# First Strassen pair: T3's split ahead of T1's, its convolution next and the gelu behind; a head's last norms and transposes behind the next key projection

## The chip, the cores and the metric

The kernel runs on one core of one Trainium2 chip. The metric is the time of one execution in device microseconds; the time before is the median of three runs. Its engines are called PE (TensorE, matmuls), DVE (VectorE), ACT (ScalarE), POOL (GpSimd) and SP (SyncE, which only issues transfers here). Each engine works through its own list of instructions in order, and waits by semaphores for the others.

## The reference

One layer of a decoder with a hybrid mixer, for a prompt of 1024 tokens and for 8 sample sequences of 8 tokens each; the width is 1024, D_FF is 2816.

```python
h  = rmsnorm(x, pre_mix_g)
proj = h @ w_in                                   # q, k, v, gates of 4 retention and 4 mLSTM heads
ret_y = head_groupnorm(retention(q_r, k_r, v_r), ret_g) * silu(g_r)
ml_y  = head_groupnorm(mlstm(q_m, k_m, v_m, gates), ml_g) * sigmoid(o_m)
x = x + rmsnorm(concat(ret_y, ml_y) @ w_out, post_mix_g)
up = rmsnorm(x, pre_ffn_g) @ w_up                 # 2 * D_FF columns
conv = sum(padded[:, j:j + L] * conv_w[j] for j in range(3)) + conv_b    # causal, each column alone
gate, val = conv[..., :D_FF], conv[..., D_FF:]
x = x + rmsnorm((gelu(gate) * val) @ w_down, post_ffn_g)
```

The new states of the heads and the last rows of the convolution are outputs too.

## The kernel before

**Numbers.** Every operand of a big matmul is split in two parts, high (h) and low (l), and a product is the sum of three matmuls: high by high, high by low and low by high. A split is two instructions: ACT writes the high part (line 148), DVE the low part as a difference (line 150). So a weight `wh_up`/`wl_up` costs ACT and DVE one instruction each, and T1 to T4, sums of activations, are split in the same way in two halves each (`T1h`, `T1l`, ...).

**The heads.** `mix_head` works through the heads r0 to r3 (retention) and m0 to m3 (mLSTM). It projects the head's q, k (and v) first: `proj` computes four blocks of tokens, 24 matmuls each (line 164), in one of two PSUM banks in turn, and an evacuation by ACT or DVE empties each. Then come nine chunks of 128 tokens in the order `[[0, 1], [2, 3], [4, 5], [6, 7], [8]]`; chunk 8 holds the sample's tokens. `stats` gathers mean and variance, and `finish` closes a group of four chunks, or the sample: it computes the norm's factors, scales each chunk on DVE (line 682, `on_...`), transposes it on PE (line 684, `yt_...`) and evacuates it into `yT`. Each `finish` is called one step late. So the group of chunks 4 to 7 is finished behind the sample's step, and the sample's at the head's end; both were called ahead of the next head's projections.

**The order.** A scheduler merges the program as it is written into a list for each engine, when the kernel is built: where an instruction has to wait, others that come later in the text can be set ahead of it. `tc.issue_after(x)` binds an instruction behind x. The order is then fixed. It also picks which of a pool's PSUM banks a tile gets.

**The up-projection.** Columns of `w_up` are worked on in pairs j = 0 to 21: a gate tile (`Ug`) and a value tile (`Uv`). Pairs 0 and 1 (`firsts`, `plain`) are plain products. From pair 2 on, each pair is a Strassen-Winograd scheme of seven products (`prods`), with two halves of 12 matmuls each, in the order A11, A12, S2, S1, S4, S3, A22, times the activations B1, B2, T2, T1, B3, T3, T4 (lines 1079 to 1081; the trace names them `up_A` or `up_S` by the weight). Each half takes one of eight PSUM banks (`psF`). A11's are evacuated by ACT into `Uv` (line 1064), the others by DVE's additions into `Ug` and `Uv` (lines 1053 and 1057). The U tiles are double buffered: pair 2 writes into pair 0's, so its evacuations wait until pair 0's convolution has read them.

**What follows a pair.** `convs` convolves `Ug`, applies the gelu on ACT (line 1098; the first one needs a table load, as other functions were in use) and convolves `Uv`. A convolution is an ACT instruction (line 1092) and two DVE passes (line 1094), each for the prompt (1024 elements) and the sample (64). `pair_out` multiplies gate by value (`act`, line 1103) and sends it away (`bd`); every second pair, differences on GpSimd (line 1111) are sent too.

**Around the change.** The products A11 and A12 of pair 2 are issued first (`held`), while the activations are still summed. Then the text has the splits of T2 and T1, a weight, the convolutions of pair 0, the split of T3, the other weights, T4, and the outputs of pairs 0 and 1, before the loop over pairs from 2 on. `last["acc"]` and `last["sq"]` name the DVE and ACT instruction behind which the next splits are bound.

Of the kernel before, what the change touches and what calls it, by code (L numbers as in the profile page):

```python
# [16 lines left out]
P = 128  # L17
# [79 lines left out]
def hybrid_layer_kernel(ctx: ExitStack, tc: tile.TileContext, a: dict, o: dict):  # L97
# [63 lines left out]
    def product(ps, w, x, b, k, term):  # L161

        u, v = ((w[0], 0), (w[1], 0), (w[0], 1))[term]
        nc.tensor.matmul(ps, u[:, k * P:(k + 1) * P], x[b // 2][k // 4][v][:, k % 4, qcols(b)],  # L164
                         start=k == term == 0, stop=k == KT - 1 and term == 2)

    def dense(ps, w, x, b):

# [367 lines left out]

    EARLY = (0, 1, 2, 3)
    turns = {"wq": 0}
    early = []

    def mix_head(hd, ml):

# [10 lines left out]
        if ml:  # L553
            proj((16 + hd, evac_norm(q, 1.0)))
            proj((20 + hd, evac_norm(k, SCALE)))
            proj((24 + hd, evac_copy(v)))
        else:
            eq, ek = evac_rot(q, f"q{nm}"), evac_rot(k, f"k{nm}")
            if hd == 0:
                proj((0, eq), mid=pre_norm, banks=lambda i, b: psB)  # L560
                proj((NH, ek))
            else:
                proj((hd, eq))
                proj((NH + hd, ek))
            if hd == 0:
                token_norms()
                yT.extend(flat("yT", i, k=2) for i in range(4))
            if hd > 1:
                proj((2 * NH + hd, evac_copy(v)))
            if hd == 0:  # L570
                gate_proj()
                for _ in range(5):
                    next(rows)
                for i in range(NH):
                    proj((12 + i, early_gate(i)), banks=lambda i, b: psB if b % 2 else psA)
                    next(rows)
# [80 lines left out]
                nc.vector.bn_stats(st, on[:, i, :P])  # L657
                nc.vector.bn_aggr(mv[:, i, :], st)

        def finish(on, mv, c0, L, name):  # L660

            sh = [P, L]
            small = lambda tag: m2.tile([P, 4], F32, tag=tag, name=f"{tag}_{name}")[:, :L]
# [17 lines left out]
            for i in range(L):  # L681
                nc.vector.tensor_scalar(on[:, i, :P], on[:, i, :P], mv[:, i, 0:1], A[:, i:i + 1],
                                        ALU.subtract, ALU.mult)
                nc.tensor.transpose(ps[:, i * P:(i + 1) * P], on[:, i, :P], ident)
# [9 lines left out]
        def sample(kz, vt, qs, pt):  # L694
# [28 lines left out]
            nc.sync.dma_start(o["cs" if ml else "ss"][hd].rearrange("p (s v) -> p s v", s=NB), sb[:, :, :P])  # L723
            if ml:
                nc.sync.dma_start(o["ns"][hd], sb[:, :, P])
            return lambda: finish(on, mv, 8, 1, f"{nm}s")

        S = None
        g = math.exp(CH * LG[hd])
# [2 lines left out]
        def pair_of(c0, kz, vt, qs, pt):  # L732
# [23 lines left out]
                S = S2  # L756
            stats(on, po, c0 % 4, 2, mv, f"{nm}{c0}")
            if c0 % 4 == 2:
                return lambda: finish(on, mv, c0 - 2, 4, f"{nm}{c0}")

        todo = None
        order = [[0, 1], [2, 3], [4, 5], [6, 7], [8]]
# [1 line left out]
        for i, cs in enumerate(order):  # L764
            cur, ready = ready, front(order[i + 1]) if i + 1 < len(order) else None
            done = sample(*cur) if cs == [8] else pair_of(cs[0], *cur)
            if todo:
                todo()
            todo = done
            next(rows, None)  # L770
            if hid > 2 or i % 2 == 0:
                next(wsums, None)
        nc.sync.dma_start(o["cp" if ml else "sp"][hd], S)
        todo()


    sd = dr.tile([JT, P, 4, D // 2], F32, name="sd")
# [259 lines left out]
    def up_products(j, ws):  # L1037
# [21 lines left out]
        def add_s3(i, ps):  # L1059
# [1 line left out]
            add(rows[1], 0, i, ps)  # L1061

        prods = {
            "A11": ("B1", lambda i, ps: nc.scalar.activation(first(i), ps, AF.Copy)),  # L1064
            "A12": ("B2", lambda i, ps: add(rows[0], 0, i, ps, first(i))),
            "S2": ("T2", lambda i, ps: add(rows[1], 0, i, ps)),
            "S1": ("T1", lambda i, ps: add(rows[1], 1, i, ps, first(i))),
# [18 lines left out]
    def conv(U, C, jt):  # L1086
        nc.gpsimd.tensor_copy(cache[:, jt, 0, :], U[:, LP:LP + 2])
        nc.gpsimd.tensor_copy(cache[:, jt, 1:, :], seq(U[:, 2 + LP:UW])[:, :, LS:])
        cw = lambda i: vec[:, V_CW + 44 * i + jt:V_CW + 44 * i + jt + 1]
        own = seq(U[:, 2 + LP:UW])  # L1090
        for c, u in ((C[:, :LP], lambda i: U[:, i:i + LP]), (seq(C[:, LP:]), lambda i: own[:, :, i:i + LS])):
            nc.scalar.activation(c, u(2), AF.Identity, scale=cw(2), bias=vec[:, V_CB + jt:V_CB + jt + 1])  # L1092
            for i in (1, 0):
                nc.vector.scalar_tensor_tensor(c, u(i), cw(i), c, ALU.mult, ALU.add)  # L1094

    def convs(j, ug, uv):
        conv(ug, cs_[:, 0, :], j)
        last["gelu"] = nc.scalar.activation(cs_[:, 0, :], cs_[:, 0, :], AF.Gelu_apprx_tanh)
        conv(uv, cs_[:, 1, :], JT + j)

    def pair_out(j):
# [371 lines left out]
```

## Time and profile before

| | |
|---|---|
| median of three runs | 1342.87 us (1345.44, 1341.48, 1342.87) |
| the profiled execution, its own time | 1343.25 us |
| its span in the trace | 1341.5 us |
| PE busy | 1318.0 us, 98% |
| DVE busy | 998.1 us, 74% |
| ACT busy | 596.5 us, 44% |
| GpSimd busy | 433.9 us, 32% |
| mean granted clock of TensorE | 0.995 |

The profiled execution's time is 1.75 us longer than its span, which is what lies around the program. Times in the trace count from the span's start. A row of a timeline gives start, duration, engine, line, operation and tiles (out <- in); in square brackets stands how long the engine had been idle, and what ended that. A row of several equal instructions (x2) gives the time from the first's start to the last's end. Instructions overlap a little, so the step from one start to the next is the cost of one in a full queue.

### The profile page before, as it was taken

Reading aid. Unit: us, or ns where it says so; the run is one execution under the profiler, and the core shown is the slowest. Engines: PE = TensorE matmul, PEld = TensorE weight load, DVE = VectorE, ACT = ScalarE, POOL = GpSimd, SP = SyncE. Lnnn points to the kernel's source line nnn. Section 1 sums busy time; section 2 is a strip of 40 time slices with the busy share of each in tenths; the row PEclk is TensorE's granted clock in tenths of the full one; section 3 lists DMA queues with packets and bytes.
Section 4 is the critical chain, followed back from the end, with each engine's and each line's share of the span. In section 5 each row is a group of like instructions: output and inputs, shape, how many; then the busy total and the mean of one; then the engine's idle time right before and its main releaser. Section 6 shows DMA issues by size and latency. Waiting matters only on the chain.

```text
span 1341.5 us, 26943 instructions
## 1 busy us (share of the span) xinstructions
PE 1318.0 (98%) x10607; PEld 1304.6 (97%) x10607; DVE 998.1 (74%) x2020; ACT 596.5 (44%) x1125; POOL 433.9 (32%) x565
## 2 busy tenths in 40 slices
PE   9999999999999999999989999999999999999996
PEld 8999999999999999999989999999999999999995
DVE  6878876447566467577799887877878788996677
ACT  7545433313323337355464343443434455453563
POOL 0345441688773000001143212232122205972002
PEclk9999999999999999999999999999999999999998
DMA  6433542576874214224034434333343359533363
GB/s 241 136 117 126 164 154 71 174 233 211 220 178 142 64 50 152 95 71 161 17 124 157 153 120 145 140 134 137 120 145 138 130 185 326 173 94 96 96 217 133
DMA packets 92734, 192.58 MB, mean 144 GB/s; under 512 B 16192, under 2 KB 41408, under 8 KB 92096
## 3 DMA queue, kind: packets, MB, share of 16 engines
q1 hardware_dynamic: 80304, 148.80, 33.2%
q0 software_dynamic: 12160, 41.95, 10.2%
q8 instruction: 83, 1.36, 0.4%
q14 instruction: 43, 0.35, 0.1%
q10 hardware_dynamic: 144, 0.11, 0.0%
HBM read 134.36 MB, written 56.47 MB: 142 GB/s over the span
## 4 chain that ended last, share of the span: by engine, by line
PE 90%; DVE 6%; ACT 1%; issue 1%; DMA 1%; SPq 0%; DVEq 0%; ACTq 0%
PE in L164 26%; PE out L164 7%; PE up_S L1081 6%; PE up_S L1079 6%; PE up_S L1080 6%; PE up_A L1080 5%; PE up_A L1079 4%; PE up_A L1081 4%; PE dn L1290 4%; PE dn L1291 4%; PE dn L1292 4%; PE up_A L1126 1%; PE up_A L1127 1%; PE up_A L1125 1%; DVE rb L1219 1%
## 5 line engine op out<-in xcount | busy, mean ns | idle before, releaser
L164 PE MATMUL in<-hh,wh_in 128*128 128x272 f32 x1024 | 299.0, 294 | 2.1 <-ACT wh_in L148 1.6
L164 PE MATMUL in<-hl,wh_in 128*128 128x272 f32 x1024 | 297.1, 292 | 0.0
L164 PE MATMUL in<-hh,wl_in 128*128 128x272 f32 x1024 | 294.8, 290 | 0.0
L164 PEld LDWEIGHTS in<-hh,wh_in 128*128 128x128 f32 x1024 | 192.4, 188 | 5.8 <-issue 2.3
L164 PEld LDWEIGHTS in<-hh,wl_in 128*128 128x128 f32 x1024 | 192.5, 189 | 0.6 <-issue 0.3
L164 PEld LDWEIGHTS in<-hl,wh_in 128*128 128x128 f32 x1024 | 192.2, 188 | 0.3 <-DVE hl L229 0.2
L148 ACT ACTIVATE wh_up<-st_up 128x1024 fp32r<-128x1024 f32 x84 | 80.4, 959 | 164.1 <-PE up_S L1080 91.3
L1219 DVE TENSOR_TENSOR rb<-rb 128x544 fp32r<-128x544 f32 x78 | 78.0, 1005 | 34.3 <-ACT rb L1218 33.1
L150 DVE TENSOR_TENSOR wl_up<-st_up,wh_up 128x1024 fp32r<-128x1024 f32 x84 | 96.9, 1156 | 8.8 <-ACT wh_up L148 8.8
L1053 DVE TENSOR_TENSOR Uv<-Uv,up_S 128x272 f32<-128x272 f32 (+1 forms) x200 | 66.7, 378 | 46.1 <-PE up_S L1081 46.1
L1111 POOL TENSOR_TENSOR act<-act 128x544 f32<-128x544 f32 x40 | 65.4, 1635 | 64.0 <-DMA bd<-act 49.0
L1239 POOL TENSOR_TENSOR wd<-wd 128x512 f32<-128x512 f32 x44 | 75.1, 1735 | 32.0 <-issue 13.8
L1218 ACT ACTIVATE rb<-rb 128x544 fp32r<-128x544 f32 x78 | 50.5, 650 | 74.8 <-DMA rb<-bd 64.6
L789 POOL TENSOR_TENSOR tab<-tab 128x256 f32<-128x256 f32 x104 | 79.5, 775 | 11.6 <-DMA tab<-in_wu 7.1
L1094 DVE SCALAR_TENSOR_TENSOR c<-Uv,vec,c 128x1024 f32<-128x1024 f32 (+1 forms) x88 | 69.3, 792 | 9.7 <-ACT c L1092 9.7
L1044 POOL MEMSET Ug<- 128x2 f32 x22 | 2.2, 99 | 219.3 <-DMA xr<-in_x 110.1
L1094 DVE SCALAR_TENSOR_TENSOR c<-Ug,vec,c 128x1024 f32<-128x1024 f32 x88 | 68.9, 819 | 0.0
L789 POOL TENSOR_TENSOR wq<-wq 128x256 f32<-128x256 f32 x56 | 52.0, 939 | 46.4 <-DMA wq<-in_wu 44.2
L1092 ACT ACTIVATE c<-Ug,vec 128x1024 f32<-128x1024 f32 (+1 forms) x44 | 34.6, 834 | 52.1 <-DVE Ug L1057 46.9
L789 POOL DMA_DIRECT2D tab<-in_wu x52 | 36.8, 713 | 49.8 <-DVE k_r L508 36.1
L150 DVE TENSOR_TENSOR wl_in<-st_in,wh_in 128x1024 fp32r<-128x1024 f32 (+2 forms) x33 | 41.3, 1251 | 13.1 <-ACT wh_in L148 13.0
L1079 PE MATMUL up_S<-B3h,wh_up 128*128 128x272 f32 x160 | 46.8, 293 | 3.7 <-ACT Uv L1064 3.7
(566 smaller groups left out, 4611.2 us busy)
## 6 DMA issues: line engine op xcount, KB each, us to landing
rb<-bd SPq DMA_DIRECT2D x76, 272.0 KB, 2.8
st_up<-sd SPq DMA_DIRECT2D x40, 512.0 KB, 3.8
bd<-act SPq DMA_DIRECT2D x33, 544.0 KB, 4.4
st_in<-in_wi SPq DMA_DIRECT2D x31, 512.0 KB, 4.3
tab<-in_wu POOLq DMA_DIRECT2D x52, 256.0 KB, 4.7
sd<-tab POOLq DMA_DIRECT2D x26, 512.0 KB, 3.8
st_up<-in_wu SPq DMA_DIRECT2D x24, 512.0 KB, 3.3
wd<-in_wd SPq DMA_DIRECT2D x44, 256.0 KB, 5.0
```

The source lines that it names most:

```text
L148: act = nc.scalar.activation(hi, x, AF.Copy)
L150: last["split"] = act, eng.tensor_tensor(lo, x, hi.bitcast(F32), ALU.subtract)
L164: nc.tensor.matmul(ps, u[:, k * P:(k + 1) * P], x[b // 2][k // 4][v][:, k % 4, qcols(b)], start=k == term == 0, stop=k == KT - 1 and term ...
L789: last["sums"] = f(*args)
L1053: nc.vector.tensor_tensor(o_, o_ if x is None else c(x), c(ps), ALU.add)
L1079: nc.tensor.matmul(ps, wh[:, c], xh[:, k, n], start=k == 0, stop=False)
L1080: nc.tensor.matmul(ps, wh[:, c], xl[:, k, n], start=False, stop=False)
L1081: nc.tensor.matmul(ps, wl[:, c], xh[:, k, n], start=False, stop=k == 3)
L1094: nc.vector.scalar_tensor_tensor(c, u(i), cw(i), c, ALU.mult, ALU.add)
L1111: (nc.gpsimd if j + 1 < JT else nc.vector).tensor_tensor(o_, x, y, ALU.subtract)
L1219: nc.vector.tensor_tensor(lo, x, hi.bitcast(F32), ALU.subtract)
L1239: nc.gpsimd.tensor_tensor(quad(p, out), quad(p, x), quad(p, y), op)
```

## The change

It has two parts, one for the heads and one for the first Strassen pair.

**Heads.** The two last `finish` steps of every head but the last are put into `held_back` rather than called, and called behind the next head's key projection. Their transposes are bound behind the last product of that projection's block 3 (`last["product", 3]`). The norms on DVE aren't bound.

```diff
+    def finish_previous():
+        for f in held_back:
+            f(last["product", 3])
+        held_back.clear()
...
             proj((20 + hd, evac_norm(k, SCALE)))
+            finish_previous()
             proj((24 + hd, evac_copy(v)))
...
-                nc.tensor.transpose(ps[:, i * P:(i + 1) * P], on[:, i, :P], ident)
+                with tc.issue_after(after.ins) if after else nullcontext():
+                    nc.tensor.transpose(ps[:, i * P:(i + 1) * P], on[:, i, :P], ident)
...
-            if todo:
+            if todo and i + 1 == len(order) and hid + 1 < 2 * NH:
+                held_back.append(todo)
+            elif todo:
                 todo()
...
-        todo()
+        if hid + 1 < 2 * NH:
+            held_back.append(todo)
+        else:
+            todo()
```

For retention heads `finish_previous()` stands behind `proj((NH + hd, ek))` in the same way.

PE, at the end of m2's key projection (`in_3` is its block 3; `yt_m_...` are the transposes of m1's chunks 4 to 7, `yt_m1s` the sample's), has these rows before the change:

```order
L684 MATMUL yt_m_4888<-cst,on_m_4733 128x128
L164 MATMUL in_3_5126<-hh_189,wl_in_5045 128x272
L684 MATMUL yt_m_4888<-cst,on_m_4733 128x128
L164 MATMUL in_3_5126<-hl_190,wh_in_5044 128x272
L684 MATMUL yt_m_4888<-cst,on_m_4733 128x128
L164 MATMUL in_3_5126<-hh_191,wh_in_5044 128x272
L164 MATMUL in_3_5126<-hh_191,wl_in_5045 128x272
L164 MATMUL in_3_5126<-hl_192,wh_in_5044 128x272
L164 MATMUL in_3_5126<-hh_191,wh_in_5044 128x272
L164 MATMUL in_3_5126<-hh_191,wl_in_5045 128x272
L684 MATMUL yt_m1s<-cst,on_m1s 128x128
L164 MATMUL in_3_5126<-hl_192,wh_in_5044 128x272
```

PE's rows at the same place after the change:

```order
L164 MATMUL in_3_5074<-hh_191,wh_in_4992 128x272
L164 MATMUL in_3_5074<-hh_191,wl_in_4993 128x272
L164 MATMUL in_3_5074<-hl_192,wh_in_4992 128x272
L692 MATMUL yt_m_5119<-cst,on_m_4733 128x128 x4
L692 MATMUL yt_m1s<-cst,on_m1s 128x128
L164 MATMUL in_0_5158<-hh_146,wh_in_5154 128x272
L164 MATMUL in_0_5158<-hh_146,wl_in_5155 128x272
```

The five transposes moved from among the block's matmuls to a place behind all of them, as one group.

**First Strassen pair.** T3 is split ahead of T1; both convolutions of pair 0 follow T1 and one weight, without the gelu; the other weights' and T4's splits are bound behind the last convolution pass. The gelu, pair 0's output, and pair 1's convolutions and output now stand in `finish_plain`, called behind pair 2's A11 inside the loop, with the gelu bound behind ACT's evacuation of A11.

```diff
-            "A11": ("B1", lambda i, ps: nc.scalar.activation(first(i), ps, AF.Copy)),
+            "A11": ("B1", lambda i, ps: last.update(evac=nc.scalar.activation(first(i), ps, AF.Copy))),
...
     difference("T2", 4)
+    last["sq"], last["acc"] = last["split"]
+    difference("T3", 6)
+    last["sq"], last["acc"] = last["split"]
     difference("T1", 10)
     last["sq"], last["acc"] = last["split"]
     next(prep)
     cs_ = flat("c", 3, k=2)
-    convs(0, *firsts[0][2])
-    difference("T3", 6)
+    for c, u in enumerate(firsts[0][2]):
+        conv(u, cs_[:, c, :], JT * c)
+    last["acc"] = last["conv"]
     for _ in prep:
         pass
...
-    for j, _, rows in firsts:
-        if j:
-            convs(j, *rows)
-        pair_out(j)
+
+    def finish_plain():
+        with tc.issue_after(last["evac"].ins):
+            gelu()
+        pair_out(0)
+        convs(1, *firsts[1][2])
+        pair_out(1)
+
     for j in range(PLAIN, JT):
...
                 for i in range(2):
                     (held.pop(0) if held else product(name, i))()
+                if j == PLAIN and name == "A11":
+                    finish_plain()
```

DVE, from T1's or T3's split on (`wl_up_1` to `wl_up_3` are low weights of pair 2, `c` the convolution's output, `Ug_7915` and `Uv_7918` pair 0's tiles), has these rows before the change:

```order
L150 TENSOR_TENSOR T1l<-mo_6817,T1h 128x4x272 x2
L150 TENSOR_TENSOR wl_up_1_8492<-st_up_1_8489,wh_up_1_8491 128x1024
L150 TENSOR_TENSOR T3l<-mo_6818,T3h 128x4x272 x2
L150 TENSOR_TENSOR wl_up_2_8522<-st_up_2_8519,wh_up_2_8521 128x1024
L1094 SCALAR_TENSOR_TENSOR c_8495<-Ug_7915,vec,c_8495 128x1024
L1094 SCALAR_TENSOR_TENSOR c_8495<-Ug_7915,vec,c_8495 128x64
L1094 SCALAR_TENSOR_TENSOR c_8495<-Uv_7918,vec,c_8495 128x1024
L1094 SCALAR_TENSOR_TENSOR c_8495<-Uv_7918,vec,c_8495 128x64
L150 TENSOR_TENSOR wl_up_3_8528<-st_up_3_8525,wh_up_3_8527 128x512
L1094 SCALAR_TENSOR_TENSOR c_8495<-Ug_7915,vec,c_8495 128x1024
L1094 SCALAR_TENSOR_TENSOR c_8495<-Ug_7915,vec,c_8495 128x64
L150 TENSOR_TENSOR T4l<-mo_6819,T4h 128x4x272
```

DVE's rows from T3's split on after the change:

```order
L150 TENSOR_TENSOR T3l<-mo_6818,T3h 128x4x272 x2
L150 TENSOR_TENSOR T1l<-mo_6817,T1h 128x4x272 x2
L150 TENSOR_TENSOR wl_up_1_8498<-st_up_1_8495,wh_up_1_8497 128x1024
L1107 SCALAR_TENSOR_TENSOR c_8501<-Ug_7915,vec,c_8501 128x1024
L1107 SCALAR_TENSOR_TENSOR c_8501<-Ug_7915,vec,c_8501 128x64
L1107 SCALAR_TENSOR_TENSOR c_8501<-Uv_7918,vec,c_8501 128x1024
L1107 SCALAR_TENSOR_TENSOR c_8501<-Uv_7918,vec,c_8501 128x64
L1107 SCALAR_TENSOR_TENSOR c_8501<-Ug_7915,vec,c_8501 128x1024
L1107 SCALAR_TENSOR_TENSOR c_8501<-Ug_7915,vec,c_8501 128x64
L1107 SCALAR_TENSOR_TENSOR c_8501<-Uv_7918,vec,c_8501 128x1024
L1107 SCALAR_TENSOR_TENSOR c_8501<-Uv_7918,vec,c_8501 128x64
L150 TENSOR_TENSOR wl_up_2_8521<-st_up_2_8518,wh_up_2_8520 128x1024
```

T3l moved ahead of T1l, and the convolution's four passes stand together behind one weight; two weights, once between and ahead of passes, stand behind them.

ACT, at the evacuation of pair 2's A11 (`Uv_...<-up_A_...`; `wh_up_0` and `wh_up_1` are weights of pair 3), has these rows before the change:

```order
L148 ACTIVATE T4h<-mo_6819 128x4x272 x2
L148 ACTIVATE wh_up_0_8577<-st_up_0_8575 128x1024
L148 ACTIVATE wh_up_1_8640<-st_up_1_8638 128x1024
L1098 ACT_TABLE_LOAD
L1098 ACTIVATE c_8495<-c_8495 128x1088
L1064 ACTIVATE Uv_8568<-up_A_8417 128x272
L1064 ACTIVATE Uv_8568<-up_A_8430 128x272
```

ACT's rows at the same place after the change:

```order
L148 ACTIVATE T4h<-mo_6819 128x4x272 x2
L148 ACTIVATE wh_up_0_8577<-st_up_0_8575 128x1024
L1077 ACTIVATE Uv_8540<-up_A_8417 128x272
L1077 ACTIVATE Uv_8540<-up_A_8430 128x272
L1110 ACT_TABLE_LOAD
L1110 ACTIVATE c_8501<-c_8501 128x1088
L148 ACTIVATE wh_up_1_8640<-st_up_1_8638 128x1024
```

The two evacuations moved ahead of the table load, the gelu and one weight.

With other times of release the scheduler also gives out other banks: pair 3's first S2 product (the first row with T2h of that pair on PE) waited for DVE before, and waits for ACT after the change.

Line numbers behind line 540 differ between the two programs: the gelu's line 1098 is 1110 after the change, the convolution's 1092 and 1094 are 1105 and 1107, and A11's evacuation, 1064, is 1077.

More of the change, by code (lines that the diff above doesn't have):

```diff
@@ L163, in product @@
         u, v = ((w[0], 0), (w[1], 0), (w[0], 1))[term]
-        nc.tensor.matmul(ps, u[:, k * P:(k + 1) * P], x[b // 2][k // 4][v][:, k % 4, qcols(b)],
-                         start=k == term == 0, stop=k == KT - 1 and term == 2)
+        last["product", b] = nc.tensor.matmul(ps, u[:, k * P:(k + 1) * P], x[b // 2][k // 4][v][:, k % 4, qcols(b)],
+                                              start=k == term == 0, stop=k == KT - 1 and term == 2)
     def dense(ps, w, x, b):
@@ L538, in hybrid_layer_kernel @@
     turns = {"wq": 0}
-    early = []
+    early, held_back = [], []
+    def finish_previous():
+        for f in held_back:
+            f(last["product", 3])
+        held_back.clear()
     def mix_head(hd, ml):
@@ L564, in mix_head @@
                 proj((NH + hd, ek))
+                finish_previous()
             if hd == 0:
@@ L658, in stats, with finish @@
                 nc.vector.bn_aggr(mv[:, i, :], st)
-        def finish(on, mv, c0, L, name):
+        def finish(on, mv, c0, L, name, after=None):
             sh = [P, L]
@@ L725, in sample @@
                 nc.sync.dma_start(o["ns"][hd], sb[:, :, P])
-            return lambda: finish(on, mv, 8, 1, f"{nm}s")
+            return lambda after=None: finish(on, mv, 8, 1, f"{nm}s", after)
         S = None
@@ L758, in pair_of @@
             if c0 % 4 == 2:
-                return lambda: finish(on, mv, c0 - 2, 4, f"{nm}{c0}")
+                return lambda after=None: finish(on, mv, c0 - 2, 4, f"{nm}{c0}", after)
         todo = None
@@ L1093, in conv, with gelu @@
             for i in (1, 0):
-                nc.vector.scalar_tensor_tensor(c, u(i), cw(i), c, ALU.mult, ALU.add)
+                last["conv"] = nc.vector.scalar_tensor_tensor(c, u(i), cw(i), c, ALU.mult, ALU.add)
+    def gelu():
+        last["gelu"] = nc.scalar.activation(cs_[:, 0, :], cs_[:, 0, :], AF.Gelu_apprx_tanh)
     def convs(j, ug, uv):
         conv(ug, cs_[:, 0, :], j)
-        last["gelu"] = nc.scalar.activation(cs_[:, 0, :], cs_[:, 0, :], AF.Gelu_apprx_tanh)
+        gelu()
         conv(uv, cs_[:, 1, :], JT + j)
@@ L1178, in hybrid_layer_kernel @@
     acts_ = flat("act", 2, k=2)
-    for j, _, rows in firsts:
-        if j:
-            convs(j, *rows)
-        pair_out(j)
+    def finish_plain():
+        with tc.issue_after(last["evac"].ins):
+            gelu()
+        pair_out(0)
+        convs(1, *firsts[1][2])
+        pair_out(1)
     for j in range(PLAIN, JT):
```

## The prediction

> **What bounds the kernel now.** I read the page first: how busy each engine is, and the clock that TensorE was granted. Columns of the first rows are busy microseconds, share of the span and instructions.
>
> ```profile
> span 1341.5 us, 26943 instructions
> PE 1318.0 (98%) x10607; PEld 1304.6 (97%) x10607; DVE 998.1 (74%) x2020; ACT 596.5 (44%) x1125; POOL 433.9 (32%) x565
> ```
>
> TensorE (PE) is busy for 1318.0 of 1341.5 us. All that a change of order can win lies in the other 23.5 us and in stretches at a low clock; no matmul is removed here. So the second view is the list of what PE waited for (us in total, times, longest), the rows of the code that the change touches:
>
> ```profile
> PE up_S L1079 <- ACT Uv L1064: 3.7, 1, 3.7
> ...
> PE yt_m1s L684 <- DVE on_m1s L682: 0.7, 1, 0.7
> PE yt_m0s L684 <- DVE on_m0s L682: 0.6, 1, 0.6
> PE yt_r L684 <- DVE on_r L682: 0.4, 1, 0.4
> ```
>
> The change aims at these four: 3.7 us at one place in the first Strassen pair, 1.7 us in the heads. Third, PE's own timeline at the 3.7 us (start, duration, line, operation):
>
> ```profile
> 678.24 0.29 PE L1081 MATMUL up_S<-T1h,wl_up 128*128 128x272 f32 x1
> 682.26 0.40 PE L1079 MATMUL up_S<-B3h,wh_up 128*128 128x272 f32 x1 [3.73 <-ACT Uv L1064]
> 682.50 0.29 PE L1080 MATMUL up_S<-B3l,wh_up 128*128 128x272 f32 x1
> 682.62 0.29 PE L1081 MATMUL up_S<-B3h,wl_up 128*128 128x272 f32 x1
> ...
> 683.68 0.43 PE L1080 MATMUL up_S<-B3l,wh_up 128*128 128x272 f32 x1
> 683.91 0.43 PE L1081 MATMUL up_S<-B3h,wl_up 128*128 128x272 f32 x1
> ...
> 686.63 0.43 PE L1081 MATMUL up_S<-B3h,wl_up 128*128 128x272 f32 x1
> ```
>
> Normally a matmul follows the last after 0.125 us (682.50 to 682.62). Here the step from 678.24 to 682.26 is 4.02, so 3.89 us are lost (I use 0.13 for a step). From 683.68 the steps are 0.23. Fourth, the windows of the granted clock (busy us of PE, PEld, DVE, ACT and POOL, then the clock):
>
> ```profile
> 676.72:680.13 3.41, 1.81 (x15) 1.59 (x13) 3.41 (x5) 2.81 (x4) 1.28 (x3) 1.00 0.23 77
> 680.13:683.55 3.42, 1.29 (x10) 1.29 (x11) 3.42 (x5) 2.36 (x4) 2.64 (x2) 1.00 0.00 0
> 683.55:686.96 3.41, 3.41 (x17) 3.41 (x17) 3.41 (x7) 0.70 (x1) 0.77 (x1) 0.50 0.69 222
> ```
>
> After a stretch in which PE was busy for 1.29 of 3.42 us, the clock was 0.50 for one stretch; after one with 1.81 it stayed at 1.00. Fifteen steps of 0.228 instead of 0.125 us lose 1.55 us. The place costs 3.89 + 1.55 = 5.44 us.
>
> **The pair, what goes.** PE's matmul at 682.26 writes a PSUM bank that ACT has to empty (evacuate) first. ACT's timeline there, and in the second pair:
>
> ```profile
> 678.44 1.06 ACT L148 ACTIVATE wh_up<-st_up 128x1024 fp32r<-128x1024 f32 x1 [0.58 <-PE up_S L1080]
> 679.52 1.28 ACT L1098 ACT_TABLE_LOAD   x1
> 680.81 1.11 ACT L1098 ACTIVATE c<-c 128x1088 f32<-128x1088 f32 x1
> 681.83 0.67 ACT L1064 ACTIVATE Uv<-up_A 128x272 f32<-128x272 f32 x2
> ...
> 699.02 1.06 ACT L148 ACTIVATE wh_up<-st_up 128x1024 fp32r<-128x1024 f32 x1 [2.96 <-PE up_A L1080]
> 699.99 0.38 ACT L1064 ACTIVATE Uv<-up_A 128x272 f32<-128x272 f32 x1
> ```
>
> The evacuation at 681.83 stands behind the gelu (table load 1.28, gelu 1.11), which itself waits for the convolution on DVE. After the change the evacuation stands ahead of the gelu, and needs only the second convolution, whose input tile it reuses. When does that end? DVE's timeline:
>
> ```profile
> 666.25 2.50 DVE L150 TENSOR_TENSOR T1l<-mo,T1h 128x1088 fp32r<-128x1088 f32 x2 [2.42 <-ACT T1h L148]
> ...
> 669.79 2.49 DVE L150 TENSOR_TENSOR T3l<-mo,T3h 128x1088 fp32r<-128x1088 f32 x2
> 672.20 1.22 DVE L150 TENSOR_TENSOR wl_up<-st_up,wh_up 128x1024 fp32r<-128x1024 f32 x1
> 673.33 1.48 DVE L1094 SCALAR_TENSOR_TENSOR c<-Ug,vec,c 128x1024 f32<-128x1024 f32 x2
> ...
> 676.12 0.69 DVE L150 TENSOR_TENSOR wl_up<-st_up,wh_up 128x512 fp32r<-128x512 f32 x1
> 676.72 1.48 DVE L1094 SCALAR_TENSOR_TENSOR c<-Ug,vec,c 128x1024 f32<-128x1024 f32 x2
> 678.11 1.29 DVE L150 TENSOR_TENSOR T4l<-mo,T4h 128x1088 fp32r<-128x1088 f32 x1
> 679.31 1.48 DVE L1094 SCALAR_TENSOR_TENSOR c<-Uv,vec,c 128x1024 f32<-128x1024 f32 x2
> ...
> 684.17 0.79 DVE L1053 TENSOR_TENSOR Ug<-Uv,up_A 128x272 f32<-128x272 f32 x2
> ```
>
> DVE idled 2.42 us ahead of T1l; T3l (2.49) now stands there, and T1l still ends at about 668.8. Its first reader, S1's first T1 product, starts four halves of a 12-matmul product before S4's place at 678.4, at about 675.3, so moving T3 ahead costs nothing while T1 comes up to 6 us later. One weight split (1.1 us, start to start 672.20 to 673.33) brings DVE to 669.9, the four convolution passes (1.4 us each, 673.33 and on) to about 675.7. ACT can evacuate at about 676.1 to 676.8; PE needs the bank at 678.4. The whole 3.73 us and, with no window under half busy, the half clock go: -5.44. Margin: 1.6 us.
>
> **The pair, what comes.** DVE has been full there, so what stood between the passes now stands behind them: two weight splits (1.1 and 0.6), T4l (2.4 in two parts), a split of the next pair (1.1), then the evacuation of A12 into Ug, first half 0.4. From 675.7 that adds up to 681.3. S4's low weights come at 676.8, before its 678.4. S3's first half needs A12's bank, and PE gets there 24 steps behind 678.4, at 681.4. So the new wait is between 0 and 0.5; I take 0.2. A22, 24 steps on at 684.4, needs T4l (679.8) and banks that DVE clears behind the pair's output: 0 to 0.3, I take 0.1. The gelu, the outputs and their transfers, moved behind A11, keep their old place ahead of the second convolution, so ACT has over 4 us for them; nobody on PE reads them in this pair.
>
> In the second pair (j=3), the bank of the first S2 product is now one which ACT frees by evacuating that pair's own A11, where DVE's work freed it before. That evacuation stands on ACT behind a weight split that waits for A12's last matmul (699.02 above): PE, done with A12, waits from about 699.0 until 699.99 + 0.38 + 0.04 for the signal, 1.4 us. The lower bound is 0 (the scheduler's bank is free by another path), the upper 2.0. I take 1.4, which these rows give. A12 of that pair needs banks which DVE clears behind convolution passes:
>
> ```profile
> 690.37 2.20 DVE L1094 SCALAR_TENSOR_TENSOR c<-Uv,vec,c 128x1024 f32<-128x1024 f32 x1
> 692.49 1.27 DVE L1094 SCALAR_TENSOR_TENSOR c<-Ug,vec,c 128x1024 f32<-128x1024 f32 x1
> ```
>
> The first pass ran beside GpSimd's subtraction and took 0.93 longer than the second; if such a pass falls ahead of an evacuation, 0 to 0.9, I take 0.4. New waits: 0.2 + 0.1 + 1.4 + 0.4 = 2.1 (bounds 0 and 3.7). The pair gives -5.44 + 2.1 = -3.3.
>
> A wait of 1.4 us leaves a window at least 2.0 of 3.41 busy, above the 1.81 that kept the clock. The Trainium skill has a rule that speaks against this change (TensorE: Matmul & The Clock Gate, "A second HAM failure mode: psum-queue depth-cycling"): short idle times between groups of matmuls, as banks are cycled, can make the clock swing between its two states. One long wait becomes several short ones, so the rule has a rival of its own below; no row of this trace shows such a swing.
>
> **The heads.** A head's last norms (DVE) and transposes (PE) were called so that the transposes fell among the next projections' matmuls. Two rows of DVE, one of PE and two windows of PE (busy us):
>
> ```profile
> 386.91 2.19 DVE L682 TENSOR_SCALAR on_m<-on_m,mv_m,A_m 128x128 f32<-128x128 f32 x4
> ...
> 389.87 0.83 DVE L682 TENSOR_SCALAR on_m1s<-on_m1s,mv_m1s,A_m1s 128x128 f32<-128x128 f32 x1
> ```
>
> ```profile
> 390.85 0.30 PE L684 MATMUL yt_m1s<-cst,on_m1s 128*128 128x128 f32 x1 [0.73 <-DVE on_m1s L682]
> ```
>
> ```profile
> 387.80:391.20 3.40, 2.40 (x17) 1.00 1.36 99
> 439.30:442.70 3.40, 3.40 (x30) 1.00 0.00 0
> ```
>
> At m1 PE loses 1.00 us of the stretch, 0.73 at the sample's transpose and 0.27 at the other four. Now all five wait for the key projection's last product: the four stand 15 products (15 x 0.126 = 1.9 us) later, the sample's 7 (0.9 us). DVE's rows keep their order, so the sample's norm is still done at 390.70. PE would come to its transpose at 390.85 - 0.73 - 0.27 + 0.9 = 390.75: 0.1 left, 0.9 won. Behind a block of transposes without matmuls between, some of it may stay; bounds 0.4 to 0.9, I take 0.6. At m0 (0.61 waited) 0.9 us of room covers all: 0.6. At r0 the transposes move by one product: 0.1 of 0.4. At r1, r2, m2 there was no wait, and they only move later: 0. Between r3 and m0, DVE evacuates the query projection's last block now behind r3's state updates:
>
> ```profile
> 277.47 1.07 DVE L722 SCALAR_TENSOR_TENSOR sb_r<-sb_r,us_r 128x256 f32<-128x256 f32 x3
> ```
>
> Four updates of 0.36 keep its PSUM bank for 1.4 us; the projections have two banks, and the next user of that one comes a block of 24 matmuls (3.0 us) later. I take +0.3, between 0 and 0.7. Heads: -0.6 - 0.6 - 0.1 + 0.3 = -1.0 (bounds +0.7 and -1.6). The moved norms issue no transfers of their own. On the Sync queue only the first pair's output stands elsewhere, ahead of a weight fetch, with over 10 us before that weight is read.
>
> **The sum.** -3.3 - 1.0 = -4.3 us. The profiled execution took 1343.25 (span 1341.5 and 1.75 around it), 0.38 above the median of 1342.87. 1343.25 - 4.3 = 1338.95; against the median 1342.87 - 4.3 = **1338.6**. A measurement of this kernel can tell about 0.3%, 4.0 us: the bounds are 1338.8 and 1346.9, so my forecast lies just on the faster side.
>
> **The rivals.**
> - *The clock drops again once* (0.14, same). Short waits of pair 2 or 3 fall into one window with PE under about half busy. For it: 1.29 lost the clock; against it: 1.81 did not. One more half-clock window: +1.6, 1340.2.
> - *The heads give nothing* (0.13, same). The transposes as a block wait as long as before, because the norms on DVE are the end of the chain at m0 and m1 either way. +1.0: 1339.6.
> - *The convolution comes late, so the change doesn't do what it says* (0.08, same). If all four passes run at 2.20 instead of 1.28, they end 3.7 us later, at 679.4, and Ug at 685.0. S4 waits 2.1 us for its low weights at 680.5, S3 another 1.5, and the half clock returns (1.55), with 1.9 for the rest: 7.05 against 5.44. Net 1342.87 + 1.6 - 1.0 = 1343.5. GpSimd's big work, though, starts only at 690, so I hold it unlikely.
> - *No new wait* (0.13, faster). The bank of pair 3's S2 is free by another path and DVE keeps up: -5.44 - 1.0, 1336.4; with the heads' full -1.6: 1335.8.
> - *The clock swings* (0.06, slower). The place is pairs 2 and 3: waits of 0.1 to 1.4 us at S3, A22, A12 and S2 put every second window at half clock. A pair has 14 x 12 = 168 matmuls; half of two pairs' 336 at 0.103 us more each is 17 us, of one pair 8.7. It decides where PE is busy under 1.8 of 3.41 us in window after window. 1342.87 - 4.3 + 8.7 = 1347.3. Against it: the stretch at 387.80 kept clock 1.00 with 2.40 busy.
>
> **How the numbers follow.** The forecast has 0.46, of which 0.37 lies below 1338.8. Faster: 0.37 + 0.13 = 0.50. Same: 0.09 + 0.14 + 0.13 + 0.08 = 0.44. Slower: 0.06. The range goes down to the case without new waits, 1335.8, and up to 1341.8: the clock's drop at 1340.2 with the new waits at their upper bound (3.7 for 2.1). Left out are the late convolution and the swinging clock, 0.14.
>
> **What would show it.** In the profile after: no wait of PE for ACT's Uv at S4, and no clock under 1.00 between 676 and 700 (right); a wait of about 1.4 us at the second pair's first S2 product, on ACT's Uv; T3l straight behind T2l on DVE without idle time before T1l; no wait at yt_m0s and at most 0.3 at yt_m1s. I am wrong if S4 still waits by over 1 us, if a window of 0.50 appears in pairs 2 or 3, or if PE's waits at r1 to m2 sum to over 1 us.

## The result, and the profile after

The changed kernel took 1340.67 us (median of 9 runs, 1336.64 to 1341.84), the kernel before beside it 1343.95 (9 runs, 1341.48 to 1345.44). The ratio is 0.9965, with a 95% interval of 0.9953 to 0.9976: 3.2 to 6.3 us faster, 4.7 in the middle. In five further runs beside the experiments the ratio was 0.9964 (0.9951 to 0.9977). Forecast was -4.3 us, or 1338.6 us. The median lies 2.1 us above that: inside the range of 1335.8 to 1341.8, but not under the bound of 1338.8, below which the forecast had seen a chance of 0.50. The kernel before had a median of 1342.87 us over its first three runs and 1343.95 over all nine, so the absolute times say less than the ratio.

The first rows of the page (busy us, share of the span, instructions):

```profile
span 1339.3 us, 26934 instructions
PE 1317.0 (98%) x10607; PEld 1304.3 (97%) x10607; DVE 999.8 (75%) x2020; ACT 595.4 (44%) x1125; POOL 428.5 (32%) x565
```

PE's busy time fell by 1.0 us, the span by 2.2. An estimate of the 1.0 is 1.55 less in the slow matmuls around S4 and 0.65 more at the end of the program, where the clock fell in this trace ahead of the last matmuls and in the one before only behind them (under "The clock" below). Now what PE waited for, in the rows that answer to those of before:

```profile
PE u_r L749 <- ACT vts L619: 2.0, 1, 2.0
...
PE up_S L1092 <- ACT Uv L1077: 1.3, 1, 1.3
...
PE yt_m0s L692 <- ACT wh_in L148: 0.8, 1, 0.8
...
PE yt_m1s L692 <- DVE on_m1s L689: 0.3, 1, 0.3
...
PE yt_m L692 <- DVE on_m L689: 0.2, 1, 0.2
```

The row `up_S <- Uv` went from 3.7 to 1.3, but it is another place now. PE's timeline at the old place, S4 of the first Strassen pair, and at the new one, S2 of the second pair:

```profile
679.68 0.29 PE L1094 MATMUL up_S<-T1h,wl_up 128*128 128x272 f32 x1
679.81 0.29 PE L1092 MATMUL up_S<-B3h,wh_up 128*128 128x272 f32 x1
679.94 0.28 PE L1093 MATMUL up_S<-B3l,wh_up 128*128 128x272 f32 x1
...
695.36 0.29 PE L1094 MATMUL up_A<-B2h,wl_up 128*128 128x272 f32 x1
696.95 0.39 PE L1092 MATMUL up_S<-T2h,wh_up 128*128 128x272 f32 x1 [1.31 <-ACT Uv L1077]
```

S4 starts 0.13 us behind S1, without a wait. S2 of the second pair loses 1.59 - 0.13 = 1.46 us. On ACT the evacuation of A11 now stands ahead of the table load and the gelu, and in the second pair behind a weight split (start, duration):

```profile
676.24 1.06 ACT L148 ACTIVATE wh_up<-st_up 128x1024 fp32r<-128x1024 f32 x1
677.57 0.69 ACT L1077 ACTIVATE Uv<-up_A 128x272 f32<-128x272 f32 x2 [0.28 <-DVE c L1107]
678.28 1.28 ACT L1110 ACT_TABLE_LOAD   x1
679.57 1.12 ACT L1110 ACTIVATE c<-c 128x1088 f32<-128x1088 f32 x1
...
695.56 1.06 ACT L148 ACTIVATE wh_up<-st_up 128x1024 fp32r<-128x1024 f32 x1 [1.90 <-PE up_A L1093]
696.52 0.67 ACT L1077 ACTIVATE Uv<-up_A 128x272 f32<-128x272 f32 x2
```

DVE has no idle time between T2l, T3l and T1l. It then idles 0.39 us for ACT's part of the convolution, and the four passes run in one piece up to 677.46 (675.98 + 1.48), when ACT evacuates at once:

```profile
665.18 2.48 DVE L150 TENSOR_TENSOR T3l<-mo,T3h 128x1088 fp32r<-128x1088 f32 x2
667.68 2.51 DVE L150 TENSOR_TENSOR T1l<-mo,T1h 128x1088 fp32r<-128x1088 f32 x2
...
671.72 1.48 DVE L1107 SCALAR_TENSOR_TENSOR c<-Ug,vec,c 128x1024 f32<-128x1024 f32 x2 [0.39 <-ACT c L1105]
...
675.98 1.48 DVE L1107 SCALAR_TENSOR_TENSOR c<-Uv,vec,c 128x1024 f32<-128x1024 f32 x2
677.37 1.82 DVE L150 TENSOR_TENSOR wl_up<-st_up,wh_up 128x1024 fp32r<-128x1024 f32 x2
```

The clock stayed at 1.00 over both pairs (busy us of PE, PEld, DVE, ACT, POOL, then the clock):

```profile
673.00:683.00 10.00, 9.99 (x80) 9.77 (x78) 10.00 (x15) 7.86 (x13) 6.78 (x6) 1.00 0.32 115
...
693.00:703.00 10.00, 8.69 (x70) 8.47 (x69) 10.00 (x18) 5.45 (x8) 7.11 (x8) 1.00 0.56 180
```

The new row is u_r's 2.0 us, behind r0. In the order it is no new wait: DVE's and SP's instructions at r0 stand as before. In both programs ACT has `vts` behind the conversion of a table of constants (`sel`, line 379), whose load (`xsel`) goes into the tile that r0's state leaves (`out_ss`). SP's queue in the kernel before, and in the changed one (issue, duration of the issue):

```profile
150.17 0.59 SPq L723 DMA_DIRECT2D out_ss<-sb_r  x1
154.05 0.33 SPq L373 DMA_DIRECT2D xsel<-in_cx  x1
```

```profile
151.56 0.60 SPq L731 DMA_DIRECT2D out_ss<-sb_r  x1
156.81 0.34 SPq L373 DMA_DIRECT2D xsel<-in_cx  x1
```

ACT's conversion in the kernel before, and in the changed one:

```profile
157.41 1.06 ACT L379 ACTIVATE sel<-xsel 100x1024 fp32r<-100x1024 f32 x1 [0.68 <-DMA xsel<-in_cx]
```

```profile
161.85 1.06 ACT L379 ACTIVATE sel<-xsel 100x1024 fp32r<-100x1024 f32 x1 [4.32 <-DMA xsel<-in_cx]
162.81 1.12 ACT L619 ACTIVATE vts<-x_r,rcol 128x128 f32<-128x128 f32 x4
```

The state goes out 1.4 us later (DVE's small operations on it run beside GpSimd's work this time), and both transfers take longer, 5.3 us instead of 3.9 between the two issues and 5.0 instead of 3.4 from the second to ACT. Together that is 4.4 us, and PE pays 2.0 of them.

Where did the time go? I take four matmuls that every run has: the first of the gates' projection (62 us), the first of the output projection (517), the first of S2 of pair 2 (672), and the first A11 of pair 4 (714), and the differences between their starts:

| profiled run | heads | out, plain pairs | pairs 2 and 3 | the rest |
|---|---|---|---|---|
| before | 455.43 | 154.86 | 41.67 | 627.45 |
| changed | 456.32 | 155.09 | 38.32 | 627.21 |
| changed, second trace | 454.14 | 155.98 | 38.68 | 627.52 |
| only the heads' part | 452.97 | 154.88 | 41.63 | 627.22 |
| only the pair's part | 454.53 | 155.44 | 38.33 | 627.58 |
| S2: evacuation ahead of the weight | 452.52 | 155.30 | 38.12 | 628.30 |
| S2: and weights behind the convolution | 454.93 | 155.06 | 36.75 | 627.07 |
| constants ahead of r0 | 453.63 | 155.26 | 38.33 | 626.84 |
| transposes behind the value projection | 456.13 | 154.88 | 38.43 | 628.12 |
| only the gelu moved, heads as before | 454.95 | 154.88 | 39.49 | 626.44 |
| the gelu not moved | 454.85 | 154.86 | 38.43 | 626.64 |
| no sums on GpSimd | 451.21 | 155.32 | 38.37 | 627.09 |
| S2 mended and constants ahead of r0 | 452.59 | 154.83 | 36.79 | 627.52 |

The pairs' column tells the change to a few tenths: 41.6 to 41.7 without, 38.1 to 38.7 with it. The heads' column doesn't: with the same heads as before it lies between 454.5 and 455.4, with the changed heads between 452.5 and 456.3.

### The profile page after: what moved, and what is told of

Same layout as the page of the kernel before. It is cut to its first block, busy times and chain, and to the rows that moved or that the text cites. A ratio compares the mean times of both kernels' runs of the same rounds, so it can differ in the third digit from the quotient of the medians.

```text
span 1339.3 us, 26934 instructions
## 1 busy us (share of the span) xinstructions
PE 1317.0 (98%) x10607; PEld 1304.3 (97%) x10607; DVE 999.8 (75%) x2020; ACT 595.4 (44%) x1125; POOL 428.5 (32%) x565
## 4 chain that ended last, share of the span: by engine, by line
PE 90%; DVE 6%; DMA 2%; ACT 2%; issue 1%; SPq 0%; DVEq 0%; ACTq 0%
PE in L164 26%; PE out L164 7%; PE up_S L1094 6%; PE up_S L1092 6%; PE up_S L1093 6%; PE dn L1316 5%; PE dn L1317 5%; PE dn L1318 5%; PE up_A L1093 4%; PE up_A L1092 4%; PE up_A L1094 4%; PE up_A L1142 1%; PE up_A L1143 1%; PE up_A L1141 1%; DVE facc L1398 1%
## 5 line engine op out<-in xcount | busy, mean ns | idle before, releaser
L1127 POOL TENSOR_TENSOR act<-act 128x544 f32<-128x544 f32 x40 | 64.4, 1611 | 56.7 <-DMA bd<-act 41.7
L802 POOL TENSOR_TENSOR wq<-wq 128x256 f32<-128x256 f32 x56 | 48.2, 871 | 44.9 <-DMA wq<-in_wu 42.7
L148 ACT ACTIVATE wh_in<-st_in 128x1024 fp32r<-128x1024 f32 (+2 forms) x33 | 34.0, 1029 | 39.5 <-PE in L164 36.6
L1092 PE MATMUL up_S<-T2h,wh_up 128*128 128x272 f32 x160 | 46.1, 288 | 1.3 <-ACT Uv L1077 1.3
```

Of the source, the lines that this page charges most:

```text
L148: act = nc.scalar.activation(hi, x, AF.Copy)
L802: last["sums"] = f(*args)
L1092: nc.tensor.matmul(ps, wh[:, c], xh[:, k, n], start=k == 0, stop=False)
```

## The experiments

**The changed kernel once more.** No edit.

> The changed kernel once more, for a second trace of it. Theory A (the 2.2 us that PE lost at r0 in the first trace come from a transfer of constants that happened to land late; the change didn't move that): the pair again gives -3.3 us, the waits at S3 and S2 again 0.3 and 1.5, but the wait of u_r for vts is anywhere from 0 to 2.2, and the time lies 3 to 6 us under the kernel before. Theory B (the wait at r0 is the change's own): u_r waits about 2 us again.

Ratio 0.9964 (0.9951 to 0.9977). The second trace has no wait of u_r, and pairs 2 and 3 give -3.0 (38.68). The heads give -1.3. Nor has any of the six other traces with the changed heads and the table in its old place a wait of u_r. Theory A holds, B falls: the wait at r0 is not a fixed part of the change. At m0 the sample's transpose waits 0.8 us as before:

```profile
PE up_S L1092 <- ACT Uv L1077: 1.3, 1, 1.3
...
PE yt_m0s L692 <- DVE on_m0s L689: 0.8, 1, 0.8
```

**One part alone.** The heads' part, with the pair's code as before:

```diff
-    for c, u in enumerate(firsts[0][2]):
-        conv(u, cs_[:, c, :], JT * c)
-    last["acc"] = last["conv"]
+    convs(0, *firsts[0][2])
+    difference("T3", 6)
```

(with the gelu and pair 0's and 1's outputs back ahead of the loop), and the pair's part, with the heads as before:

```diff
-        if hid + 1 < 2 * NH:
-            held_back.append(todo)
-        else:
-            todo()
+        todo()
```

> Only the heads' part. Theory A: -1.0 us against the kernel before where the constants land in time, +1.2 where they land late; the stall of 3.7 us at S4 stays. Theory B: +0.9 us in every run, as the first trace summed it up to the end of the heads.

> Only the first Strassen pair's part. Theory A: -3.3 us against the kernel before, with S4's wait gone, 0.3 at S3, 1.5 at the second pair's S2. Theory B: -3.3 too, so that this part alone is better than the whole change by 0.9 us. A third reading (the heads bring nothing and the pair all of the measured gain) expects -4.7.

Heads alone: 0.9981 (0.9970 to 0.9992), 1.1 to 4.0 us faster. Its trace has no wait at any `yt`; the first row is the old one:

```profile
PE up_S L1092 <- ACT Uv L1077: 3.7, 1, 3.7
```

Pair alone: 0.9970 (0.9957 to 0.9983), 2.3 to 5.8 us faster, and 41.67 - 38.33 = 3.34 us in the trace. Theory B's +0.9 us for the heads lies outside its interval, and so does the reading that the heads bring nothing. Theory A's -1.0 lies just outside too, on the small side. The -4.7 of the third reading for the pair lies within its interval of times, but the trace's 3.34 speaks against it. The two middles, -2.6 and -4.0, add up to more than the whole (-4.7); the intervals are wide enough for that.

**The second pair's S2.** First ACT's order alone, then DVE's too:

```diff
-            split_to(x, hi, lo, nc.vector, (last["sq"], last["acc"]) if i in (1, 2) or j == 1 else None)
+            split_to(x, hi, lo, nc.vector, (last["sq"], last["conv"]) if j == PLAIN + 1 and i > 1 else
+                     (last["sq"], last["acc"]) if i in (1, 2) or j == 1 else
+                     (last["evac"], None) if j == PLAIN + 2 and i == 0 else None)
```

The first kernel has only the last of these three lines new.

> The whole change, and the weight split that stood on ACT ahead of the second pair's evacuation of A11 is bound behind it. If the wait of 1.5 us at that pair's S2 comes from that order alone, it goes, and the kernel is 1.4 us faster than the changed one. If PE then waits for that weight or for DVE, at the third pair's A11, the gain is below 0.5.

> The whole change, with the second pair's evacuation of A11 ahead of the weight split on ACT (as in the run before), and the second pair's low weights for S4, S3 and A22 bound on DVE behind pair 1's last convolution pass, 1.7 us of work that stood ahead of it. If the wait at the second pair's S2 has two layers (the order on ACT, then pair 1's convolution on DVE), it goes: -1.5 us against the changed kernel between the pair's S1 and the third pair. If DVE is simply full, it moves on to S4's low weights or to the outputs, and the gain is below 0.5.

The first: 0.9966 (0.9953 to 0.9980), 38.12 us in the pairs, only 0.2 to 0.6 under the changed kernel's traces. The wait is still 1.0 us, because the evacuation, first in its queue now, waits for pair 1's last convolution pass on DVE, and 1.7 us of splits stand ahead of that. DVE's rows, then ACT's:

```profile
689.18 1.81 DVE L150 TENSOR_TENSOR wl_up<-st_up,wh_up 128x1024 fp32r<-128x1024 f32 x2
690.92 1.46 DVE L1108 SCALAR_TENSOR_TENSOR c<-Uv,vec,c 128x1024 f32<-128x1024 f32 x2
```

```profile
692.50 0.69 ACT L1078 ACTIVATE Uv<-up_A 128x272 f32<-128x272 f32 x2 [2.51 <-DVE c L1108]
```

The second: 0.9959 (0.9945 to 0.9973), 36.75 us, 1.4 less than the first and 1.6 to 1.9 less than the changed kernel; no wait of `up_S` is left in its list. So the wait had two layers, and the one I had named was the outer one. DVE's order alone was not tried. In the changed kernel's trace it could not have been enough: DVE's last pass of pair 1 ended at 696.05 (694.59 + 1.46), the weight split on ACT only at 696.62. The weights behind the passes are not missed: nothing new waits.

**The constants at r0.** The table's load and conversion are called ahead of r0's state load.

```diff
+        if hid == 0:
+            sel_consts()
         sb = m2.tile([P, NB, 129], F32, tag="sb", bufs=1, name=f"sb_{nm}")
```

> The whole change, and the table of constants that ACT converts behind r0 is loaded and converted ahead of r0 (its tile is then free when r0's state comes in). Theory A (run-to-run: two transfers in a row, the state out and the table in, at times land 2 us too late for u_r, whatever the change): the wait of u_r for vts can't appear; the median is 0 to 1 us under the changed kernel's, and its runs spread less. Theory B (the change pushes r0's end back): the same wait appears on another engine, and the median stays.

Ratio 0.9964 (0.9950 to 0.9977), five runs of 1337.54 to 1341.15. No wait of u_r, but one trace without it shows little, as the second trace of the changed kernel had none either. That the spread is smaller is not shown: one run of five lies 3 us above the others. So this wait alone is not what sets the changed kernel's runs apart, four at 1336.6 to 1337.3 and five at 1340.7 to 1341.8. Nor are these two firm groups: its five further runs lie between them, at 1337.74 to 1340.14.

**Transposes later still.** For the mLSTM heads, behind the value projection.

```diff
-            finish_previous()
             proj((24 + hd, evac_copy(v)))
+            finish_previous()
```

> The whole change, but the mLSTM heads' last norms and transposes stand behind the value projection, 96 matmuls (12 us) later. If the waits left at m0 and m1 (0.2 to 1.0 us each) come from norms on DVE that end late, they go: -0.5 to -1.5 us over the heads. If what is left comes from the transposes themselves as a block, the time doesn't change.

The expected gain did not come: 0.9975 (0.9963 to 0.9987), and 456.13 us over the heads, within the scatter of the other traces. No transpose of an mLSTM head waits, but the projection does:

```profile
PE in L164 <- DVE k_m L499: 3.3, 3, 1.7
```

DVE still does the norms first (they aren't bound), and behind them evacuates the key projection's blocks. With the transposes gone from there, PE reaches the value projection sooner and wants a bank that DVE hasn't emptied. What was late is DVE's chain of norms; the transposes were only the first to notice it.

**The pair's two halves.** Only the gelu moved:

```diff
     difference("T2", 4)
-    last["sq"], last["acc"] = last["split"]
-    difference("T3", 6)
-    last["sq"], last["acc"] = last["split"]
     difference("T1", 10)
...
         conv(u, cs_[:, c, :], JT * c)
-    last["acc"] = last["conv"]
+    difference("T3", 6)
```

and all but the gelu:

```diff
         conv(u, cs_[:, c, :], JT * c)
+        if c == 0:
+            gelu()
...
-        with tc.issue_after(last["evac"].ins):
-            gelu()
         pair_out(0)
```

> Of the pair's part only the gelu is moved behind the evacuation of A11; T3 stays behind T1, the convolution's passes stay mixed with the splits, and the heads are as before. S4 then waits for the last convolution pass alone: from 678.4 to about 681.3, 2.8 us instead of 3.9, and the window behind it is busy for over 2.2 of 3.42 us. If the clock falls only below a share between 1.29 and 1.81 us, the half clock goes as well: -2.6 us at S4. If any wait of about 3 us trips it, -1.1.

> The whole change, but the gelu stays where it was, ahead of ACT's evacuation of A11; only T3's place and the convolution's order are new in the pair. The last pass over Ug ends at 676.1 in the changed kernel's trace and the weight split ahead of the gelu at 677.3, so table load and gelu end at 679.7, and the evacuation's first half at about 680.1, against PE's arrival at 679.8. If the convolution's order is what counts, S4 waits 0.3 to 0.6 us, and the pair gives -2.8 to -3.3 as with the gelu moved. If the gelu's place is what counts, S4 waits at least 2.0 us.

Only the gelu moved (with the heads as before): 0.9989 (0.9980 to 0.9999), pairs 39.49 us. S4 waits 2.8 us, as worked out, and the clock stays at 1.00 (its rows stand under "The clock" below):

```profile
PE up_S L1087 <- ACT Uv L1072: 2.8, 1, 2.8
```

The gain of 2.18 us is 0.9 of wait and 1.3 of clock, net of what comes new. The other half (the whole change, gelu in its old place): 0.9967 (0.9957 to 0.9978), pairs 38.43 us, as with the gelu moved. S4 loses 0.25 us:

```profile
675.20 1.28 ACT L1110 ACT_TABLE_LOAD   x1
676.49 1.11 ACT L1110 ACTIVATE c<-c 128x1088 f32<-128x1088 f32 x1
677.51 0.67 ACT L1077 ACTIVATE Uv<-up_A 128x272 f32<-128x272 f32 x2
```

Once the convolution is early, the gelu fits ahead of the evacuation. So DVE's new order is enough for the pair's gain, and moving the gelu then adds nothing that can be measured, though by itself it gave 2.18 of the 3.3 us. DVE's order has two parts, T3's place and the convolution's, which were not tried apart.

**GpSimd beside the norms.** The sums of `w_up`'s quadrants, GpSimd's arithmetic during the heads, are left out; the transfers stay. This kernel doesn't compute the reference's FFN.

```diff
-                    queued(nc.gpsimd.tensor_tensor, o_, x, y, op)
+                    pass
```

> The whole change without GpSimd's arithmetic on the sums of w_up's quadrants during the heads (it leaves the four additions and subtractions of each stretch out; the transfers stay). If the norms on DVE end late because GpSimd works beside them (four of on_m took 2.05 to 2.34 us at m0 and m1, and 1.12 at r0 beside no GpSimd work), they now take 1.2 to 1.6, no wait is left at yt_m0s and yt_m1s, and the heads gain 1.0 to 2.0 us more. If DVE's chain is late by itself, the waits of 0.3 to 0.8 stay.

Ratio 0.9956 (0.9941 to 0.9971), whose interval overlaps the changed kernel's. Heads 451.21 us, 2.9 and 5.1 less than in the two traces of the changed kernel, and 1.3 to 5.1 less than in all six with the same code in the heads. No wait is left at any `yt`. DVE's norms at m1 in this kernel, and in the changed one:

```profile
382.90 1.12 DVE L689 TENSOR_SCALAR on_m<-on_m,mv_m,A_m 128x128 f32<-128x128 f32 x4
384.32 0.35 DVE L689 TENSOR_SCALAR on_m1s<-on_m1s,mv_m1s,A_m1s 128x128 f32<-128x128 f32 x1
```

```profile
388.97 2.05 DVE L689 TENSOR_SCALAR on_m<-on_m,mv_m,A_m 128x128 f32<-128x128 f32 x4
391.80 0.84 DVE L689 TENSOR_SCALAR on_m1s<-on_m1s,mv_m1s,A_m1s 128x128 f32<-128x128 f32 x1
```

At m1 the same norms take about twice as long with GpSimd's sums as without. The Trainium skill (SBUF — State Buffer, "SBUF: two separate sides") has DVE and GpSimd take turns at a shared pair of ports, each for a whole instruction, if DVE's instruction runs in a two-port mode or has two inputs in SBUF. No row shows which mode these norms run in. The trace agrees where norms and additions fall wholly together, as at m1 in the kernel with S2's weights behind the convolution: four norms in 3.07 us beside four additions in 3.05.

```profile
386.65 3.07 DVE L689 TENSOR_SCALAR on_m<-on_m,mv_m,A_m 128x128 f32<-128x128 f32 x4
```

```profile
386.58 3.05 POOL L802 TENSOR_TENSOR tab<-tab 128x256 f32<-128x256 f32 x4
```

At m0 this is less clear. There the slow norms of the changed kernel (337.66 to 340.00) lie mostly beside GpSimd's issue of transfers (337.05 to 339.15), ahead of its additions from 339.16 on, while the same four norms took 1.18 and 1.13 us beside such an issue in two other traces. What of GpSimd's work holds them there stays open.

Where the heads scatter can be read from PE's steps between one head's first product of `x_m` and the next head's, which hold the same 288 rows of projection products each. From m2 to m3 GpSimd's sums end early, at 418.4 in the changed kernel, ahead of the norms at 438.3, and the step is 49.84 to 49.95 us in all 13 traces. From m0 to m1 and from m1 to m2 it is 49.85 to 52.63 in the twelve with the sums, and 49.86 both times without them. There is only one trace without the sums, but the step from m2 to m3 says the same in all of them: these two steps scatter because of GpSimd's work beside DVE. When GpSimd works there differs from trace to trace (its additions at m1 start at 386.6 in one, at 390.1 in another). It is not the whole scatter of the times. The six runs without the sums still lie 6.0 us apart (1334.82 to 1340.85), and the slowest had a mean granted clock of 0.994, the others 0.995 to 0.997.

**The best of them.** S2 mended, and the constants ahead of r0.

> The whole change with the second pair's wait removed (evacuation ahead of the weight split, low weights behind pair 1's convolution) and the constants' table loaded ahead of r0. The two should add up: -1.5 us from the pair, 0 to -1 from r0, so 1 to 2.5 us under the changed kernel; if the constants only were late by chance in one trace, -1.5 alone.

1336.35 us (6 runs, 1335.49 to 1342.25), ratio 0.9957 (0.9941 to 0.9974): 3.5 to 7.9 us faster than before. The pairs take 36.79 us, 1.5 to 1.9 less than changed; the heads' 452.59 lies within their scatter. That it beats the changed kernel is shown in the trace's pairs, not by the times, whose intervals overlap.

## Why the prediction was right, point by point

- **The pair, -3.3 us.** Measured: -3.0 to -3.4 in the traces of the changed kernel and of its part alone. The stall of 3.73 us and the half clock went (-5.44 together), as worked out from DVE's rows. With the program 1.44 us later at that place (673.79 against 672.35 at S2) the forecast of 675.7 for the convolution's end becomes 677.1. It ended at 677.46; the rest is DVE's 0.39 us of waiting for ACT's part of the convolution, which the sum had at nothing. ACT was done evacuating at 678.26 (677.57 + 0.69), 1.55 us ahead of S4 at 679.81: the margin of 1.6, as forecast.
- **The new waits, 2.1 us.** S3 lost 0.30 (0.2 forecast), the second pair's S2 1.46 (1.4), its A12 0.1 in the first trace and 0.4 in the second (0.4). The cause of S2's was half right: the order on ACT was one layer, DVE's convolution behind it the next.
- **The gelu.** I had put the stall's end down to both, the evacuation ahead of the gelu and the convolution brought forward. Only the second was needed, with T3's new place beside it.
- **The clock.** The step was that a window at half clock follows one with PE busy between 1.29 and 1.81 us. It holds, and the traces narrow it. The clock's two falls in the kernel before, at 683.55 and 1332.10 us, lie 190 steps of 3.413 us apart; so I count a trace's windows back from its fall at the end. With only the gelu moved, the window around S4's wait had PE busy for 1.59 us, and the clock held. At the end of the changed kernel's trace one with 1.45 was followed by half clock:

```profile
679.02:682.43 3.41, 1.59 (x12) 1.59 (x13) 3.41 (x4) 2.01 (x4) 2.03 (x2) 1.00 0.00 0
682.43:685.84 3.41, 3.37 (x27) 3.15 (x26) 3.41 (x6) 1.24 (x2) 1.38 (x1) 1.00 0.55 161
```

```profile
1323.17:1326.58 3.41, 1.45 (x12) 1.23 (x10) 3.41 (x4) 0.95 (x2) 2.06 (x1) 1.00 0.14 60
1326.58:1329.99 3.41, 2.18 (x4) 1.10 (x4) 0.94 (x3) 1.87 (x5) 0.00 (x0) 0.50 0.65 267
```

  So the length of a wait does not decide alone: that fall came with a wait of 2.17 us, and the 2.83 us at S4, which lay across two windows, brought none. PE's last matmuls, in the kernel before and in the changed one:

```profile
1329.60 1.53 PE L213 MATMUL ssqb_fin<-facc_sq,ones 128*128 128x272 f32 x4 [2.15 <-DVE facc_sq L1306]
```

```profile
1326.79 2.18 PE L213 MATMUL ssqb_fin<-facc_sq,ones 128*128 128x272 f32 x4 [2.17 <-DVE facc_sq L1332]
```

  Before, the fall came behind them. The 0.65 us between the two were in no term of the sum; in seven of the 13 traces these matmuls take 1.53 or 1.54, in six 1.71 to 2.18, whatever the kernel's order. The rule of the Trainium skill on psum-queue depth-cycling (TensorE: Matmul & The Clock Gate) would have brought the swinging clock; no trace here shows it with one wait of 1.5 us, and two of 0.1 to 0.4, in two pairs.
- **The heads, -1.0 us.** Six traces with the changed heads have a mean of 454.29 us (456.32, 454.14, 452.97, 452.52, 454.93, 454.85), three with the old ones 454.97 (455.43, 454.53, 454.95): -0.7, with a scatter of 3.8 between traces of the same code, so the traces show neither sign nor size. The runs of that part alone say -1.1 to -4.0: the sign is shown, the size is at the forecast or above it. The working failed at m0, where 0.9 us of room was to cover a wait of 0.6 us: I took the durations of one trace as given, and there the norms took 2.34 us instead of 1.59, so that the transpose waited for 0.8 us in both traces of the changed kernel. That the whole came out near -4.3 is partly luck. DVE before, DVE after, and PE after:

```profile
336.07 1.59 DVE L682 TENSOR_SCALAR on_m<-on_m,mv_m,A_m 128x128 f32<-128x128 f32 x4
```

```profile
337.66 2.34 DVE L689 TENSOR_SCALAR on_m<-on_m,mv_m,A_m 128x128 f32<-128x128 f32 x4
...
340.77 0.83 DVE L689 TENSOR_SCALAR on_m0s<-on_m0s,mv_m0s,A_m0s 128x128 f32<-128x128 f32 x1
```

```profile
341.75 0.30 PE L692 MATMUL yt_m0s<-cst,on_m0s 128*128 128x128 f32 x1 [0.77 <-ACT wh_in L148]
```

  (The profile names ACT's split, which ended at 341.64; DVE's norm ended at 340.77 + 0.83 = 341.60, and the second trace names that.) By the prediction's own test this step fails in the first trace: PE's waits at the transposes add up to 1.3 us (0.8 + 0.3 + 0.2), over the 1 us that it set. In the second they are 0.8.
- **r3 to m0, +0.3.** That was wrong, as far as the traces show. From r3's first `u_r` to m0's first `x_m` PE takes 42.34 us in the three traces with the old heads and 42.61 to 42.67 in those with the changed ones. But 260 rows of projection products stand there instead of 258, and two products are 0.25 us; between r1 and r2 they are two fewer (290 for 292). No wait is left over.
- **Slower by contention, not in my list.** The wait of 2.0 us at r0 was in no rival. It is one of chance, but the range had to carry it, and did only since it was wide for other reasons.

## What to carry to other kernels

When a wait ends with an operation that is last in a chain over two engines, look which link is late before moving things on the other engine: the evacuation stood behind the gelu, but the gelu stood behind the convolution and a weight split, and bringing the convolution forward was enough. Ask the same of the wait that comes next, since mending its outer layer alone gave 0.2 to 0.6 us of 1.5. And where small operations on one engine run beside another's stream that transfers pace, take their durations from several traces; one trace priced the heads' part to 0.1 us, and the same code scatters by 3.8.

## What the runs showed of the hardware

DVE's scaling of four 128x128 tiles took 1.12 us at m1 without GpSimd's sums, 2.05 in the changed kernel, and 3.07 where all four fell beside four GpSimd additions of 3.05 us together; the single tile took 0.35 and 0.84. A window of 3.41 us with PE busy for 1.45 us was followed by half clock, one with 1.59 was not; the waits in them were 2.17 and 2.83 us. What spreads the changed kernel's nine runs over 5.2 us (1336.64 to 1341.84) stays open: the heads' scatter in the traces is up to 3.8 us, of which the wait at r0 is 2.0 in one trace, the clock's fall at the end is 0.65, and a trace shows one run only.
